# Memory keys and values between slabs of queries, W_out fetched during pooling, a fourth raw buffer, memory values in three banks, and two moves in TensorE's order

## The chip, the cores and the metric

The kernel runs on one core of one Trainium2 chip. TensorE multiplies matrices (a stationary 128x128 tile against up to 512 moving columns) into PSUM; VectorE (DVE), ScalarE (ACT) and GpSimd (POOL) do the elementwise work; SyncE (SP) issues the transfers between the chip's memory (HBM) and the core's on-chip memory (SBUF). Times are device microseconds of one execution; lower is better.

## The reference

A decoder trunk of two layers over a sequence of 1024 tokens with 1024 channels, batch 1, in float32. Both layers project the input once (W_in, 1024 to 3072 columns: main 1024, memory queries 512, main gate 1024, memory gate 512), mix, and project back (W_out, 1536 to 1024):

```python
h = x @ w_in
y_main = main_fn(u_main)                       # layer 0: pooling, layer 1: FoX
y_mem = memory_attention(q_mem, mem, w_mem_kv) # 4 heads of 128, 256 memory tokens
y = jnp.concatenate([y_main * jax.nn.silu(g_main), y_mem * jax.nn.silu(g_mem)], axis=-1)
x = layer_norm(ALPHA * x + y @ w_out, ln_g[layer], ln_b[layer])
```

The main path of layer 0 is causal pooling: four groups of 256 channels, each the trailing mean over 2, 4, 8 or 16 tokens minus the token itself, then a 256x256 map and a scale for each channel. The main path of layer 1 is forgetting attention (FoX): 16 heads of 64 channels, causal softmax over `q_t.k_s/8 + cum[t] - cum[s]`, where `cum` is the running sum of the logarithm of a forget gate. Keys, values and gates come from one more projection of the output of layer 0. Memory attention is plain cross-attention of 4 heads into 256 memory tokens, whose keys and values are projections of `mem`.

## The kernel before

Every float32 operand is split into a high and a low part (`hi_lo`, L140-143: ACT copies the rounded high part, DVE subtracts it for the low part). A product is then three matmuls: high by high, high by low, low by high. TensorE runs 7010 matmuls, most of them with 512 columns.

**Weights.** A weight piece of 128x512 (256 KB) goes by an SP transfer into a `raw` buffer (L115-116, three of them), and is split into two `w` buffers (L118, six). `split_w` (L149) does both; in the FoX stage GpSimd does the split instead of ACT and DVE (`gp_hi_lo`, L145-147, chosen by `low[0]`). A `slab` (L171) is 48 matmuls of 512 columns: it projects 1024 tokens to 128 channels, from two weight pieces, into two PSUM banks of the kind `pj`, and calls an eviction for each half. PSUM has eight banks: `pj` three, `L` two (logits), `T` two (transposes, and FoX's exponentials), `O` one (attention outputs).

**Order of the stages.** Layer 0: `pool_group(0)`; `mem_kv(0)` (L197), which projects the memory tokens to keys of four heads and then to values of four heads, 24 matmuls of 256 columns for each (`project`, 192 in a row), evicts the keys by `hi_lo` and the values by `scaled_halves` (L231), and turns the values by one transposing transfer (L228); `mem_attention(0)` (L259), which projects four slabs of queries and then runs eight query tiles; `pool_group(1)` to `(3)` (L461-504); the output projection `OutProj(0)`. Layer 1: `mem_kv(1)`, `mem_attention(1)`, then `start_units` (keys, queries, first values and forget gates of FoX), the FoX loop, and `OutProj(1)`.

**Memory attention.** For each query tile `probs` makes logits of four heads, exponentials and two half-precision halves of the probabilities (L294 is DVE's part), which a transfer turns. `values` (L302) multiplies them by the memory values for two tiles and a head in bank `O`, and DVE evicts with L310. Between those, TensorE is given pieces of gate slabs from a list, `Fill`; gate evictions are an ACT tanh and a DVE multiply (L192-195).

**Output projection.** `OutProj.load` (L335) takes 24 W_out pieces into `raw` and splits them into tiles that lie in slots that other tiles have left (`w_slots`). `rest` (L378) loads all that are missing, then goes over pairs of token tiles: 144 matmuls for each pair, in the order of the channel groups 2 (memory), 0, 1. In layer 0 all of it happens after pooling. In layer 1 the first eight pieces and the first memory products (`early`, L364) are put into the last two FoX heads.

**FoX.** The loop goes over 16 heads and eight query tiles from the longest down. For each tile GpSimd writes the causal mask into the row `R` of that head (L682; `R` is the running gate sum broadcast to all partitions, loaded by L670 from `cumd`, two buffers), TensorE makes the logits in bank `L`, DVE adds `R` and takes the running extreme (L689), ACT exponentiates (L695), one step later ACT and DVE make two halves (L712, L713), SP turns them (L722), and TensorE multiplies by the values. The spare room on TensorE is filled from `Fill` with slabs: keys, queries and values of the next pair (queries evicted by L638 and L639), and gates. At an odd head's end the list is emptied. For pair 0 the list holds gate 0, gate 1 and then `following`, the slab of pair 1's queries. In pair 7 three gates that had no room earlier come late (`late_gate`, L752: the stored output is read back, multiplied by its gate on GpSimd in one operation of 1024 columns, L756, and stored).

**Forget gates** (`forget_gates`, L594-615): DVE ends with L597; TensorE makes the running sum (L605, L607), DVE copies it, TensorE turns it (L611), SP writes `cumd` in eight transfers (L615). `start_units` (L654) steps this chain among slab matmuls.

**What sets the order.** TensorE's order in memory attention, `start_units` and the FoX loop is the program's own (`manual_schedule`). The other engines, SP and the rest of TensorE's work are ordered by a scheduler that sees the whole program; every engine runs its instructions in the order given, so an instruction that waits holds up what is behind it. SP issues all transfers in one such order.

Of the kernel before, what the change touches and what calls it, by code (L numbers as in the profile page):

```python
# [9 lines left out]
F32 = mybir.dt.float32  # L10
# [8 lines left out]
P = 128  # L19
# [6 lines left out]
MH = 4  # L26
# [45 lines left out]
def trunk_kernel(ctx, tc, x, xT, memT, win, wk, wv0, wv, wmk, wmv, wout, poolw, pscale, lng, lnb, bforget, out):  # L72
# [11 lines left out]
    for _ in range(4):  # L84
        nc.vector.memset(small.tile([P, 8], F32, tag="edge", name="edge"), 0.0)
# [29 lines left out]
    def raw(shape):  # L115
        return sb(list(shape), "raw", 3)
# [4 lines left out]
    def tiny(n, dt=F32):  # L121
        return small.tile([P, n], dt, tag=f"s{n}{dt}", name=nm("s"))
# [40 lines left out]
    edge = const.tile([P, 40], F32, name="edge")  # L163
# [33 lines left out]
    def mem_kv(l):  # L197
        mh = [T([P, 4, NMEM]) for _ in range(2)]
# [20 lines left out]
        for h in range(MH):  # L219
            hi_lo(kh[:, h, :], kl[:, h, :], project(wmk[l, h]))  # L220
        two, v = (MK([P, MH, 2 * 2, P], F16) for _ in range(2))
        undo = small.tile([P, 64], F32, tag="undo", name=nm("undo"), bufs=1)[:, :MH]
        for h in range(MH):
# [4 lines left out]
        nc.sync.dma_start_transpose(v.rearrange("p h b d -> p (h b) d"), two.rearrange("p h b t -> p (h b t)"))  # L228
        return kh, kl, v, undo
# [29 lines left out]
    def mem_attention(l, XH, XL, kv, qtile, ytile, yd):  # L259

        kh, kl, v, undo = kv
        qs = []
        for h in range(MH):
            qh, ql = qtile(), qtile()
            run(slab(win[l, 8 + h], XH, XL, lambda cols, acc: hi_lo(qh[:, cols], ql[:, cols], acc)))
            qs.append((qh, ql))
        ys, gs = [ytile() for _ in range(MH)], [G() for _ in range(MH)]
# [34 lines left out]
        def values(c, h):  # L302
            acc = ps([P, 2 * P], "O", 1)
# [23 lines left out]
    class OutProj:  # L327
# [4 lines left out]
        def __init__(self, l, wtile, yd):  # L332
            self.l, self.wtile, self.yd, self.ws, self.accs, self.n = l, wtile, yd, [{}, {}], None, 0

        def load(self, upto):  # L335

            for n in range(self.n, upto):
# [4 lines left out]
                r = raw([P, NH])  # L342
                nc.sync.dma_start(r, wout[self.l, nh, 2 * kk + j])
                hi_lo(h[j], lo[j], r)
            self.n = max(self.n, upto)
# [18 lines left out]
        def early(self, tiles):  # L364

            yh, yl = tiles
            for j in range(2):
                r, two = raw([P, 2, 2 * P]), slice(2 * j, 2 * j + 2)
                nc.sync.dma_start(r, self.yd[2, :, two, : 2 * P])
                hi_lo(yh[:, two, :], yl[:, two, :], r)  # L370

            def units():
                self.accs = self.open()
                yield from self.products(self.accs, 2, yh, yl)

            return units()

        def rest(self, resid, XH, XL, dst):  # L378
            self.load(24)
# [125 lines left out]

# [384 lines left out]
```

## Time and profile before

| | us |
|---|---|
| three runs | 1284.34, 1287.81, 1289.43 |
| median | 1287.81 |
| the profiled execution | 1289.07 |
| its span in the trace | 1287.3 |
| TensorE busy | 1251.9 (97%) |
| VectorE busy | 801.4 (62%) |
| ScalarE busy | 579.2 (45%) |
| GpSimd busy | 168.8 (13%) |

The profile is of one execution. A row of its timeline gives start, length, engine, line, operation, `out<-in`, sizes, a count, and in brackets the idle time before it and what ended that. A row of waits gives an engine and line, what it waited for, and the total, the number of times and the longest, in us. A row of windows gives a stretch, its length, the busy time of each engine with its count of instructions, the clock that TensorE was granted (1 is full), the share of time that the transfer engines were busy, and GB/s. `SPq` is SP issuing a transfer. Names of tiles such as `pj`, `L`, `O`, `raw`, `w`, `R` are those of the program. Lengths of neighbouring matmuls overlap, so the spacing of starts tells a matmul's price better than its length.

### The profile page before, as it was taken

The numbers are of one execution on the slowest core, as the hardware profiler recorded it, in microseconds if no ns is written. First come the engines' busy times: TensorE is split into PE (matmuls) and PEld (weight loads), VectorE is DVE, ScalarE is ACT, GpSimd is POOL, SyncE is SP. The second block draws the span as 40 slices with busy tenths as digits, with TensorE's granted clock in tenths as the row PEclk, the third lists the DMA queues.
The fourth block names the chain that finished last, engine by engine and source line by source line (L and its number), as shares of the span: only waits on it lengthen the run. The fifth ranks groups of instructions, "written<-read, shape, count | busy, mean of one in ns | idle before, by whom it ended". The sixth has DMA issues, their size and how long they took to land. (4 is left out here: it accounts for less than half of the span.)

```text
span 1287.3 us, 19678 instructions
## 1 busy us (share of the span) xinstructions
PE 1251.9 (97%) x7018; PEld 1036.6 (81%) x7018; DVE 801.4 (62%) x1905; ACT 579.2 (45%) x1273; POOL 168.8 (13%) x267
## 2 busy tenths in 40 slices
PE   9999999999999999999999999999999999999997
PEld 7888878888778889887887788887888777788885
DVE  6452656355565457267456777777777887674644
ACT  5332642232331124265225667766766776653110
POOL 0000000000000000000003334333334231420000
PEclk9999999999999999999999999999999999999999
DMA  6351343212474226234516866868778786986430
GB/s 221 115 148 50 92 98 114 82 56 91 158 243 137 92 91 183 64 82 112 169 47 157 160 153 162 192 143 172 171 163 185 164 187 155 230 200 200 164 115 33
DMA packets 267426, 178.65 MB, mean 139 GB/s; under 512 B 212288, under 2 KB 225728, under 8 KB 267328
## 3 DMA queue, kind: packets, MB, share of 16 engines
q1 hardware_dynamic: 267328, 177.40, 52.0%
q8 instruction: 55, 0.90, 0.3%
q14 instruction: 43, 0.35, 0.1%
HBM read 94.97 MB, written 22.61 MB: 91 GB/s over the span
## 5 line engine op out<-in xcount | busy, mean ns | idle before, releaser
L181 PE MATMUL pj<-A,w 128*128 128x512 f32 x2928 | 726.5, 396 | 1.0 <-POOL w L147 0.6
L181 PEld LDWEIGHTS pj<-A,w 128*128 128x128 f32 x2928 | 539.5, 189 | 105.8 <-ACT A L142 1.8
L143 DVE TENSOR_TENSOR w<-raw,w 128x512 fp32r<-128x512 f32 x106 | 72.9, 689 | 117.0 <-ACT w L142 115.5
L142 ACT CAST w<-raw 128x512 fp32r<-128x512 f32 x106 | 65.6, 621 | 162.4 <-PE pj L181 103.7
L695 ACT ACTIVATE T<-MK,s 128x512 f32<-128x512 f32 x192 | 110.8, 577 | 56.6 <-DVE s L689 43.3
L713 DVE SCALAR_TENSOR_TENSOR P<-T,s,P 128x512 f16<-128x512 f32 x192 | 111.5, 613 | 34.5 <-ACT P L712 32.9
L712 ACT ACTIVATE P<-T,s 128x512 f16<-128x512 f32 x192 | 102.6, 576 | 48.2 <-issue 20.9
L169 PE MATMUL L<-B,B 128*128 128x512 f32 (+3 forms) x384 | 93.1, 346 | 13.9 <-DVE s L689 11.6
L169 PEld LDWEIGHTS L<-B,B 128*128 128x128 f32 x384 | 70.0, 188 | 36.2 <-DVE s L689 20.9
L689 DVE CUSTOM_DVE_ANT_0 MK<-L,R 128x512 f32<-128x512 f32 (+3 forms) x128 | 72.9, 570 | 15.9 <-PE L L169 10.7
L601 POOL MEMSET G<- 128x128 f32 x1 | 0.2, 205 | 620.3 <-DVE V L324 620.3
L169 PEld LDWEIGHTS <-V 128*128 128x128 f16 x1152 | 65.9, 99 | 17.9 <-issue 17.4
L169 PE MATMUL O<-T,V 128*128 128x128 f16 x1152 | 77.0, 222 | 0.0
L147 POOL TENSOR_TENSOR w<-raw,w 128x512 fp32r<-128x512 f32 x54 | 69.8, 1292 | 3.9
L142 ACT CAST T<-T 128x1024 fp32r<-128x1024 f32 x23 | 24.2, 1051 | 93.4 <-DMA T<-y1d 49.3
L682 POOL TENSOR_SCALAR_AFFINE_SELECT R<-R 128x128 f32<-128x128 f32 x128 | 40.4, 318 | 190.4 <-DVE s L689 107.7
L143 DVE TENSOR_TENSOR T<-T,T 128x1024 fp32r<-128x1024 f32 x23 | 28.1, 1220 | 58.1 <-PE L L358 41.6
L146 POOL TENSOR_SCALAR w<-raw 128x512 fp32r<-128x512 f32 x54 | 36.4, 675 | 143.6 <-PE pj L181 131.7
L213 PE MATMUL pj<-T,w 128*128 128x256 f32 x384 | 48.9, 285 | 2.7 <-ACT w L142 2.1
L213 PEld LDWEIGHTS pj<-T,w 128*128 128x128 f32 x384 | 46.9, 191 | 4.3 <-ACT w L142 2.8
L358 PE MATMUL pj<-B,T 128*128 128x512 f32 x186 | 46.5, 392 | 0.8 <-DVE B L143 0.8
L358 PE MATMUL L<-B,T 128*128 128x512 f32 x174 | 42.5, 389 | 0.0
(212 smaller groups left out, 1599.9 us busy)
## 6 DMA issues: line engine op xcount, KB each, us to landing
raw<-in_win_dram SPq DMA_DIRECT2D x96, 256.0 KB, 2.7
raw<-in_wout_dram SPq DMA_DIRECT2D x48, 256.0 KB, 3.3
B<-B SPq DMA_DIRECT2D x32, 256.0 KB, 3.9
R<-cumd SPq DMA_DIRECT2D x16, 512.0 KB, 4.3
y0d<-Y SPq DMA_DIRECT2D x12, 512.0 KB, 2.7
T<-y0d SPq DMA_DIRECT2D x12, 512.0 KB, 4.3
T<-y1d SPq DMA_DIRECT2D x11, 512.0 KB, 4.5
raw<-in_wmk_dram SPq DMA_DIRECT2D x16, 256.0 KB, 2.7
```

The costliest lines, as they stand in the source:

```text
L142: nc.scalar.copy(hi, src)
L143: nc.vector.tensor_tensor(lo, src, hi.bitcast(F32), ALU.subtract)
L147: nc.gpsimd.tensor_tensor(lo, src, hi.bitcast(F32), ALU.subtract)
L169: nc.tensor.matmul(acc, a, b, start=i == 0, stop=i == len(terms) - 1)
L181: nc.tensor.matmul(accs[n], a[:, k, :], b[:, kt, n * NH : (n + 1) * NH], start=kt == 0 and i == 0, stop=kt == KT - 1 and i == 2,)
L213: nc.tensor.matmul(acc, w[:, k, :], m[pc][:, k, :], start=pc == 0 and k == 0 and i == 0, stop=pc == 1 and k == 3 and i == 2,)
L358: nc.tensor.matmul(accs[a][nh], y[:, k, a * P : (a + 1) * P], w, start=kt == 8 and i == 0, stop=kt == 7 and i == 2,)
L682: nc.gpsimd.affine_select(R[:, qs], R[:, qs], [[-1, P]], ALU.is_ge, -NEG, base=0, channel_multiplier=1)
L689: nc.vector.tensor_tensor_reduce(p[:, lo:up], lg, R[:, lo:up], 1.0, top, ALU.add, ALU.min, m[:, n : n + 1])
L695: nc.scalar.activation(e, p[:, lo:up], AF.Exp, bias=top, scale=-1.0, accum_out=sums[:, n, hd % 2, i : i + 1],)
L712: nc.scalar.activation(pair[:, lo:up], e, AF.Copy, scale=r)
L713: nc.vector.scalar_tensor_tensor(pair[:, L + lo : L + up], e, r, pair[:, lo:up], ALU.mult, ALU.subtract)
```

## The change

- `raw` has four buffers instead of three. Room comes from smaller constant tiles: four `edge` tiles and their memsets go, `tiny` tiles of 12 columns or more have two buffers, `undo` moves.
- `mem_kv` hands out `keys(h)` and `vals(h)`. In layer 0 each slab of memory queries is followed by that head's keys and values; in layer 1 all keys come first, and each slab is followed by that head's values. The turning transfer is issued after the last head's values.
- Memory `values` use bank `O` for head 1 only, and the two `T` banks for the others.
- `OutProj.load` becomes `fetch` (the transfer) and `split`. In layer 0 four pieces are split after pooling group 1, and up to twelve after groups 2 and 3, with the slots reordered: the first six tiles lie in `B` and `W`.
- In `start_units`, nine of pair 1's query matmuls come before the running sum of the gates, and 30 instead of 39 at the end.
- In pair 0 of FoX the list holds gate 0, `following`, gate 1.
- The late gates multiply on GpSimd in four pieces of 256 columns.
- In pair 7 W_out pieces are fetched ahead of their split, and `early` is stepped: two loads and two splits at steps 7, 9, 10 and 12.

```diff
     pool = ctx.enter_context(tc.tile_pool(name="pool", bufs=2))
     small = ctx.enter_context(tc.tile_pool(name="small", bufs=4))
     psum = ctx.enter_context(tc.tile_pool(name="psum", bufs=2, space=bass.MemoryType.PSUM))
-    for _ in range(4):
-        nc.vector.memset(small.tile([P, 8], F32, tag="edge", name="edge"), 0.0)
     dram = ctx.enter_context(tc.tile_pool(name="dram", bufs=1, space=bass.MemoryType.DRAM))
     count, low = [0], [False]
...
         return sb(list(shape), "MK", 4, dt)
     def raw(shape):
-        return sb(list(shape), "raw", 3)
+        return sb(list(shape), "raw", 4)
     def wt(shape):
         return sb(list(shape), "w", 6, F32R)
     def tiny(n, dt=F32):
-        return small.tile([P, n], dt, tag=f"s{n}{dt}", name=nm("s"))
+        return small.tile([P, n], dt, tag=f"s{n}{dt}", name=nm("s"), bufs=4 if n < 12 else 2)
     def w_slots(tags, where):
...
         nc.vector.memset(invc[:, t : t + 1], 1.0 / (t + 1))
     psc = const.tile([P, 8], F32, name="psc")
     pschalf = const.tile([P, 8], F32, name="pschalf")
-    edge = const.tile([P, 40], F32, name="edge")
+    edge = const.tile([P, 32], F32, name="edge")
     nc.vector.memset(edge, 0.0)
     def mm3(acc, terms):
...
         nc.vector.scalar_tensor_tensor(dst, dst, 1.0, acc, ALU.add, ALU.mult)
     def mem_kv(l):
         mh = [T([P, 4, NMEM]) for _ in range(2)]
         ml = [T([P, 4, NMEM]) for _ in range(2)]
         for q in range(4):
...
                         )
             return acc
-        for h in range(MH):
+        two, v = (MK([P, MH, 2 * 2, P], F16) for _ in range(2))
+        undo = const.tile([P, 8], F32, tag="undo", name=nm("undo"), bufs=1)[:, :MH]
+        def keys(h):
             hi_lo(kh[:, h, :], kl[:, h, :], project(wmk[l, h]))
-        two, v = (MK([P, MH, 2 * 2, P], F16) for _ in range(2))
-        undo = small.tile([P, 64], F32, tag="undo", name=nm("undo"), bufs=1)[:, :MH]
-        for h in range(MH):
+        def vals(h):
             scaled_halves(
                 project(wmv[l, h]), [two[:, h, 2 * e : 2 * e + 2, :].rearrange("p m t -> p (m t)") for e in range(2)],
                 undo[:, h : h + 1],
             )
-        nc.sync.dma_start_transpose(v.rearrange("p h b d -> p (h b) d"), two.rearrange("p h b t -> p (h b t)"))
-        return kh, kl, v, undo
+            if h == MH - 1:
+                nc.sync.dma_start_transpose(v.rearrange("p h b d -> p (h b) d"), two.rearrange("p h b t -> p (h b t)"))
+        return (kh, kl, v, undo), keys, vals
     def scaled_halves(u, halves, un, by_tile=lambda t: t):
...
     def mem_attention(l, XH, XL, kv, qtile, ytile, yd):
-        kh, kl, v, undo = kv
+        (kh, kl, v, undo), keys, vals = kv
         qs = []
+        if l:
+            for h in range(MH):
+                keys(h)
         for h in range(MH):
             qh, ql = qtile(), qtile()
             run(slab(win[l, 8 + h], XH, XL, lambda cols, acc: hi_lo(qh[:, cols], ql[:, cols], acc)))
             qs.append((qh, ql))
+            if not l:
+                keys(h)
+            vals(h)
         ys, gs = [ytile() for _ in range(MH)], [G() for _ in range(MH)]
         pt, fill = {}, Fill()
         for h in range(MH):
...
             )
         def values(c, h):
-            acc = ps([P, 2 * P], "O", 1)
+            acc = ps([P, 2 * P], *(("O", 1) if h == 1 else ("T", 2)))
             for j in range(2):
                 t = pt[2 * c + j]
                 mm3(acc[:, j * P : (j + 1) * P], [
...
         KKS = (4, 5, 0, 1, 2, 3)
         def __init__(self, l, wtile, yd):
-            self.l, self.wtile, self.yd, self.ws, self.accs, self.n = l, wtile, yd, [{}, {}], None, 0
-        def load(self, upto):
-            for n in range(self.n, upto):
+            self.l, self.wtile, self.yd, self.ws, self.accs = l, wtile, yd, [{}, {}], None
+            self.raws, self.n = [], 0
+        def fetch(self, upto):
+            while self.n + len(self.raws) < upto:
+                n = self.n + len(self.raws)
+                r = raw([P, NH])
+                nc.sync.dma_start(r, wout[self.l, n // 2 % 2, 2 * self.KKS[n // 4] + n % 2])
+                self.raws.append(r)
+        def split(self, upto):
+            while self.n < upto:
+                self.fetch(self.n + 1)
+                n = self.n
                 kk, nh, j = self.KKS[n // 4], n // 2 % 2, n % 2
                 if j == 0:
                     self.ws[nh][kk] = self.wtile(n // 2)
                 h, lo = self.ws[nh][kk]
-                r = raw([P, NH])
-                nc.sync.dma_start(r, wout[self.l, nh, 2 * kk + j])
-                hi_lo(h[j], lo[j], r)
-            self.n = max(self.n, upto)
+                hi_lo(h[j], lo[j], self.raws.pop(0))
+                self.n += 1
         def open(self, banks=(("pj", 3),) * 2 + (("L", 2),) * 2):
             accs = [ps([P, NH], *bank) for bank in banks]
...
                             )
                             yield NH
-        def early(self, tiles):
-            yh, yl = tiles
+        def early(self, yh, yl):
             for j in range(2):
                 r, two = raw([P, 2, 2 * P]), slice(2 * j, 2 * j + 2)
                 nc.sync.dma_start(r, self.yd[2, :, two, : 2 * P])
+                yield
                 hi_lo(yh[:, two, :], yl[:, two, :], r)
-            def units():
-                self.accs = self.open()
-                yield from self.products(self.accs, 2, yh, yl)
-            return units()
+                yield
+            self.accs = self.open()
+            yield from self.products(self.accs, 2, yh, yl)
         def rest(self, resid, XH, XL, dst):
-            self.load(24)
+            self.split(24)
             gb = []
             for v in (lng, lnb):
                 t = sb([P, D], "P", 4)
...
                     nc.vector.scalar_tensor_tensor(yn, acc, pschalf[:, f : f + 1], yn, ALU.mult, ALU.mult)
                 nc.sync.dma_start(y0d[f // 4, :, f % 4, :], ys[d])
+        wtags = [("B", 8)] * 4 + [("W", 4)] * 2 + [("MK", 4)] * 2 + [("Y", 4)] * 2 + [("PG", 0), ("w", 0)]
+        out_proj = OutProj(0, w_slots(wtags, in0), y0d)
         pool_group(0)
         kv = mem_kv(0)
         mem_attention(0, XH, XL, kv, bt, lambda: sb([P, S], "Y", 4, F32, in0), y0d[2])
         for g in range(1, 4):
             pool_group(g)
+            out_proj.split((4, 12, 12)[g - 1])
         XH1, XL1 = (sb([P, KT, S], "A", 2, F32R) for _ in range(2))
-        wtags = [("MK", 4)] * 2 + [("W", 4)] * 2 + [("B", 8)] * 4 + [("Y", 4)] * 2 + [("PG", 0), ("w", 0)]
-        OutProj(0, w_slots(wtags, in0), y0d).rest(x, XH1, XL1, x1)
+        out_proj.rest(x, XH1, XL1, x1)
     XH, XL = XH1, XL1
...
             for _ in v_turned():
                 yield from islice(own, 6)
             yield from own
+            yield from islice(following, 9)
             next(gates)
             yield from islice(following, 9)
             next(gates)
-            yield from islice(following, 39)
+            yield from islice(following, 30)
         def forget_rows(hd):
             R = sb([P, S], "R", 2, F32, in1)
...
             return R
         def probs(hd, i, R, sums, behind):
...
             o, g = sb([P, S], "R", 2, F32, in1), G()
             nc.sync.dma_start(o, y1d[pr // 4, :, pr % 4, :])
             yield from gate_units(win[1, 12 + pr], g, XH, XL)
-            nc.gpsimd.tensor_tensor(o, o, g, ALU.mult)
+            for c in range(4):
+                cols = slice(c * 2 * P, (c + 1) * 2 * P)
+                nc.gpsimd.tensor_tensor(o[:, cols], o[:, cols], g[:, cols], ALU.mult)
             nc.sync.dma_start(y1d[pr // 4, :, pr % 4, :], o)
         def fox(following, out_proj):
...
                             fill.add(pair_units(pr + 1), 3 * SLAB)
                         for ahead in {0: (0, 1), 2: (2,), 4: (4,), 7: (7,)}.get(pr, ()):
                             gate_ahead(ahead)
-                        if pr == 0:
-                            fill.add(following, SLAB)
+                            if ahead == 0:
+                                fill.add(following, SLAB)
                         for late in (3, 5, 6) if pr == 7 else ():
                             fill.add(late_gate(late), SLAB)
                     R, ahead_R = ahead_R, None
...
                         ahead_R = forget_rows(hd + 1)
                     if pr == 7:
                         step = b * ST + i
-                        out_proj.load(min(step + 1, 6) if step < 9 else 8)
-                        if step == 6:
-                            lead = out_proj.early([xy((P, 4, 2 * P)) for _ in range(2)])
+                        if step == 7:
+                            lead = out_proj.early(*(xy((P, 4, 2 * P)) for _ in range(2)))
+                        if step in (7, 9, 10, 12):
+                            next(lead)
+                        out_proj.split(min(step - 1, 6) if step < 14 else step - 7)
+                        out_proj.fetch(min(step + 1, 6) if step < 12 else min(step - 5, 8))
                     if hd < HEADS:
                         new = (hd, tile_of, o)
                         fresh[0] = probs(hd, tile_of, R, sums, behind)
```

## The prediction

> **What bounds the kernel now.** I read the page's busy shares first, then TensorE's waits, then the windows around each wait, then the timeline inside them.
>
> ```profile
> PE 1251.9 (97%) x7018; PEld 1036.6 (81%) x7018; DVE 801.4 (62%) x1905; ACT 579.2 (45%) x1273; POOL 168.8 (13%) x267
> ```
>
> TensorE sets the time. The change keeps every matmul, so only stalls in TensorE's order can be won. Two undisturbed rows give its steady rate:
>
> ```profile
> 81.57 43.71 PE L181 MATMUL pj<-A,w 128*128 128x512 f32 x192
> ```
> ```profile
> 491.91 17.04 PE L213 MATMUL pj<-T,w 128*128 128x256 f32 x140
> ```
>
> A 512-column matmul takes 43.71 / 192 = 0.228 us, a 256-column one 17.04 / 140 = 0.122 us. What a stretch takes beyond its matmuls at these rates is its loss. The waits of TensorE (total, times, longest, in us) name the causes:
>
> ```profile
> PE L L169 <- DVE s L689: 11.6, 13, 2.8
> PE O L169 <- DVE Y L310: 2.2, 2, 1.7
> PE pj L213 <- ACT w L142: 2.1, 2, 1.5
> PE O L169 <- DVE V L310: 1.9, 2, 1.7
> PE L L169 <- DVE B L639: 1.8, 1, 1.8
> PE O L605 <- DVE G L597: 1.7, 1, 1.7
> ```
>
> The stretches that the change touches, TensorE alone (window, length, busy, matmuls, granted clock, DMA share, GB/s). In order: memory keys and values of layer 0, of layer 1, first output projection, end of FoX pair 0, a later pair change left alone, head 14, memory values:
>
> ```profile
> 55.47:81.57 26.10, 24.06 (x193) 1.00 0.56 171
> 482.29:508.79 26.50, 25.71 (x210) 1.00 0.59 182
> 342.58:378.20 35.62, 34.37 (x146) 1.00 0.81 270
> 730.66:740.93 10.27, 8.47 (x51) 0.83 0.87 180
> 883.50:896.80 13.30, 10.74 (x55) 0.89 0.81 173
> 1118.15:1126.20 8.05, 5.29 (x28) 0.79 0.91 229
> 174.00:184.00 10.00, 8.28 (x73) 1.00 0.56 141
> ```
>
> Three of them have a clock below 1: a stall is followed there by slow matmuls, which go with it.
>
> **Part by part.**
>
> *Keys and values between slabs, layer 0.* 192 matmuls of 0.122 us are 23.4 us; the stretch takes 26.10, so 2.7 are lost. Why:
>
> ```profile
> L143 DVE TENSOR_TENSOR w<-raw,w 128x512 fp32r<-128x512 f32 x106 | 72.9, 689 | 117.0 <-ACT w L142 115.5
> L142 ACT CAST w<-raw 128x512 fp32r<-128x512 f32 x106 | 65.6, 621 | 162.4 <-PE pj L181 103.7
> ```
> ```profile
> raw<-in_wmk_dram SPq DMA_DIRECT2D x16, 256.0 KB, 2.7
> ```
> ```profile
> 75.23 0.50 PE L213 MATMUL pj<-T,w 128*128 128x256 f32 x2 [1.46 <-ACT w L142]
> ```
>
> A raw buffer is held for 2.7 us of landing, 0.62 of ACT and 0.69 of DVE, 4.0 in all; three buffers give a piece per 1.34 us. A projection uses two pieces in 24 x 0.122 = 2.9 us, 1.46 per piece: no slack for ACT and DVE to be late. After the change a slab (48 x 0.228 = 10.9 us) and two projections use six pieces in 16.8 us, 2.8 per piece. Bounds: -2.7 to 0. I take **-2.7**, since supply is then twice the demand. The transpose of the values on SP comes behind more weight loads, but the first use of the values is some 20 us of matmuls later in the order, so it costs nothing; without that cover it would cost its own few us.
>
> *Fourth raw buffer, layer 1.* Keys stay in a row there, values go between slabs.
>
> ```profile
> 483.24 1.06 PE L252 MATMUL T<-ident,G 128*128 128x128 f32 x8
> 484.06 4.44 PE L213 MATMUL pj<-T,w 128*128 128x256 f32 x32
> 489.09 1.92 PE L213 MATMUL pj<-T,w 128*128 128x256 f32 x12 [0.59 <-ACT w L142]
> ```
>
> 16 transposes at 1.06 / 8 are 2.1 us, so 26.50 - 23.4 - 2.1 = 1.0 us is lost here, 0.59 of it in this wait. Four buffers supply a piece per 1.0 us against 1.46. Bounds -1.0 to 0 (ACT also has the layer norm's transposes to evict): **-0.7**.
>
> *Memory values in three banks.* All L310 waits add up to 2.2 + 1.9 = 4.1 us.
>
> ```profile
> 178.82 1.17 PE L181 MATMUL pj<-A,w 128*128 128x512 f32 x4
> 181.71 0.83 PE L169 MATMUL O<-T,MK 128*128 128x128 f16 x12 [1.72 <-DVE Y L310]
> ```
> ```profile
> 179.60 1.67 DVE L294 SCALAR_TENSOR_TENSOR P<-P,s,P 128x256 f16<-128x256 f32 x4
> 181.19 0.48 DVE L310 TENSOR_SCALAR Y<-O,undo 128x256 f32<-128x256 f32 x1
> ```
>
> The bank was full at 178.82 and emptied at 181.67, 2.9 us later, because L310 queued behind L294. With banks T, O, T the fourth head waits only for the first head's eviction; between lie two heads with their fill, 2 x (0.83 + 1.17) = 4.0 us, and a further 1.17. The other banks' users (the transposes, FoX's exponentials) aren't live here. Bounds -4.1 to 0: **-4.0**.
>
> *W_out during pooling.* 342.58 to 378.20 holds 144 matmuls (146 less one overlapping at each edge), 32.8 us; 2.8 are lost. Twelve of 24 pieces, those used first, are loaded and split earlier: 12 x 0.62 ACT and 12 x 0.69 DVE, 7.4 and 8.3 us. The cover:
>
> ```profile
> 290.00:340.00 50.00, 49.85 (x220) 41.02 (x219) 27.97 (x44) 14.08 (x22) 0.00 (x0) 1.00 0.29 90
> ```
>
> (PE, PEld, DVE, ACT, POOL.) In this last pooling stretch DVE is idle for 22 us, ACT for 36, DMA share 0.29. The thirteenth to sixteenth go to MK slots that pooling's last matmuls (to 342.58) still read; they take 4 x 1.34 = 5.4 us and are first used 54 matmuls, 12.3 us, later; the last eight follow from 22 us on. Bounds -2.8 to +1 (an eviction of pooling behind two splits, 1.3): **-2.4**.
>
> *Cumulative gates: nine matmuls of pair 1 ahead of them.* The G L597 wait of 1.7 goes. What is late next is row R:
>
> ```profile
> 671.79 0.46 PE L605 MATMUL O<-G,G 128*128 128x128 f32 x2 [1.65 <-DVE G L597]
> ...
> 681.93 0.81 SPq L670 DMA_DIRECT2D R<-cumd  x2
> ...
> 687.14 0.69 DVE L689 CUSTOM_DVE_ANT_0 MK<-L,R 128x512 f32<-128x512 f32 x1 [0.93 <-DMA R<-cumd]
> ```
>
> 9 x 0.228 = 2.05 us end just when L597 does, so L605 starts no earlier, and cumd, R and L689 stay where they are. TensorE reaches FoX's first logits about 2 us sooner and waits there instead. Bounds 0 to +2 (a longer single wait, then slow matmuls): **+0.5**.
>
> *Pair 1's queries between gates 0 and 1.*
>
> ```profile
> 736.16 1.59 PE L169 MATMUL L<-B,B 128*128 128x512 f32 x4 [1.80 <-DVE B L639]
> ```
> ```profile
> 738.61 0.29 POOL L682 TENSOR_SCALAR_AFFINE_SELECT R<-R 128x128 f32<-128x128 f32 x1 [2.42 <-DMA R<-cumd]
> ```
>
> The pair's first logits waited for its query's eviction, issued last. Of the window's 10.27 us, 22 matmuls of 512 columns are 5.0 and 24 small ones, at the 0.83 / 12 of the values above, 1.7: 3.6 lost, half in the wait, half in the slow clock behind it. Earlier queries remove the wait, but GpSimd's mask of the next head, in order ahead of this head's next one, still waits for R at 738.61. Bounds -3.6 to -1.0: **-2.5**. The second gate's evictions now come last; no logits wait for them.
>
> [...]
>
> *Piece at 1088.*
>
> ```profile
> 1088.39 0.97 PE L181 MATMUL pj<-A,w 128*128 128x512 f32 x3 [0.63 <-POOL w L147]
> ```
>
> SP's load of this piece moves ahead of the value transposes: -0.6, bounds -0.9 to +0.9 (a W_out load ahead of it instead).
>
> *Head 14: fetch ahead, split later, early tiles in steps.*
>
> ```profile
> 1118.83 0.62 ACT L142 CAST B<-raw 128x512 fp32r<-128x512 f32 x1 [3.91 <-DMA raw<-in_wout_dram]
> ```
> ```profile
> 1121.53 0.51 PE L169 MATMUL L<-B,B 128*128 128x256 f32 x2 [2.76 <-DVE s L689]
> ```
>
> ACT stood 3.91 us behind a W_out transfer; L712, L713, L689 and TensorE (2.76) queue behind it. 8.05 us hold ten matmuls of 512 columns, two of 256 and 14 to 16 values, 3.6 us by the rates above: 4.5 lost. With the transfer issued at least two steps before its split, the wait goes; the split itself (0.62, 0.69) stays ahead of head 15's first exponentials. Bounds -4.5 to +2 (a split, its DVE half and the exponential behind it, still late): **-2.5**.
>
> *The rest.* Four pieces instead of one multiply on GpSimd (13% busy), at most some tenths; four memsets less: 0.
>
> Sum: -2.7 -0.7 -4.0 -2.4 +0.5 -2.5 -0.6 -2.5 = **-14.9 us**. The profiled execution took 1289.07 (span 1287.3 and 1.77 around it), 1.3 over the median 1287.81: 1274.2 on its own basis, 1272.9 on the median's. Say **1273**.
>
> **Rivals.**
>
> *A. The gains from 670 us on come back as R waits.* In FoX, L689 is already the largest wait (11.6 us), and
>
> ```profile
> POOL R L682 <- DMA R<-cumd: 54.2, 15, 8.8
> ```
>
> shows GpSimd behind R at nearly every head. If the cumulative-gate term is +2 and the last three are nothing, the sum is -2.7 -0.7 -4.0 -2.4 + 2 = -7.8: 1280. Against it: the waits at 736 and 1118 end by L639 and by a W_out transfer, not by R.
>
> *B. The changed orders make R the last wait at more heads: slower.* At 883.50 to 896.80 a change of head takes 13.3 us for 26 matmuls of 512 columns, six of 384 or fewer and some 20 values, 8.3 us: 5.0 lost, with clock 0.89. FoX has 15 changes of head; each that newly stalls so costs 5.0. Five of them give 1273 + 25 = 1298, and it is slower than now by over 0.5% (1294.2) from 21.2 / 5.0, the fifth, on. For it: GpSimd waits for R 15 times; against: only pair 0 and pair 7 change order, and between them the sequence of heads, loads and masks stays.
>
> *C. The transfers weren't the limit.* If the piece supply hangs on ACT's and DVE's queues and not on buffers, the terms of keys, W_out and head 14 go, -0.6 with them: -4.0 + 0.5 - 2.5 = -6.0, some 1282. Against: ACT's idle time names the DMA in head 14.
>
> **How the numbers follow.** This kernel's measurement can tell about 0.5%, 6.4 us. My forecast 0.57, A 0.22, C 0.11, B 0.10. The forecast's own range is 1268 (every term at its gaining bound, -2.7 - 1.0 - 4.1 - 2.8 - 3.6 - 0.9 - 4.5 = -19.6) to 1279; the range given reaches over A and C, and 3 us below for the spread of the runs: 1265 to 1284. Faster, that is under 1281.4: the forecast and 0.17 of A, 0.74; same: 0.05 of A and C, 0.16; slower: B, 0.10.
>
> **What would show it.** In the changed profile: no L213 wait on L142 over 0.5 us and 48 512-column matmuls between projections without a gap; no L310 waits; the first output projection's first 24 matmuls per bank in 5.5 us each; L605 without a wait, L689 at FoX's start still waiting for R with TensorE idle about 3 us; no L639 wait at the first pair change; no ACT wait on W_out of several us in head 14. I am wrong if these stalls are gone and L L169's waits on L689 grow by more than they save, or if pooling's evictions wait behind the W_out splits.

## The result and the profile after

The changed kernel takes 1276.09 us (median of six runs, 1273.81 to 1281.01) against 1286.81 before (six runs, 1284.33 to 1289.87): the medians lie 10.7 us apart, and the ratio is 0.9921, 95% interval 0.9895 to 0.9947. The profiled execution took 1275.16 with a span of 1273.4; it is 0.9 below its median, where the profiled one of before (1289.07) was 2.3 above. The page's busy row and the first waits of TensorE (total, times, longest, us) after the change; lines have moved (L143 is now L141, L181 L179, L169 L167, L213 L212, L310 L319, L358 L376, L597 L615, L639 L657, L689 L709, L739 L759):

```profile
PE 1243.5 (98%) x7018; PEld 1032.7 (81%) x7018; DVE 803.8 (63%) x1901; ACT 578.5 (45%) x1273; POOL 174.2 (14%) x276
```
```profile
PE L L167 <- DVE s L709: 14.1, 15, 3.1
PE idle L92 <- DVE warm L89: 1.3, 1, 1.3
PE O L167 <- DVE G L759: 1.1, 1, 1.1
PE pj L179 <- ACT A L140: 0.8, 2, 0.4
PE pj L212 <- DVE w L141: 0.8, 1, 0.8
```

Gone are the waits on the values' eviction (L310, 4.1), on the memory weights' ACT half (2.1), on the query eviction (L639, 1.8) and on the gates (L597, 1.7). The wait on L709 has grown from 11.6 to 14.1, and one on L759 is new. TensorE alone in the stretches that answer to those of before: layer 0's queries, keys and values; first output projection; layer 1's keys; memory values; end of FoX pair 0; head 14; and the last output projection's start:

```profile
56.77:123.39 66.62, 66.62 (x386) 1.00 0.36 102
337.59:370.27 32.68, 32.68 (x146) 1.00 0.69 230
474.50:500.00 25.50, 24.50 (x160) 1.00 0.49 156
171.67:178.03 6.36, 6.36 (x66) 1.00 0.52 112
706.34:716.00 9.66, 9.21 (x57) 1.00 0.52 113
1093.00:1109.00 16.00, 12.28 (x71) 0.89 0.75 197
1135.00:1157.00 22.00, 19.32 (x86) 1.00 0.84 294
```

The first, second and fourth have no idle time left. Layer 1's keys, the end of pair 0 (0.45 us), head 14 and the last output projection have.

To compare runs I took every start of a matmul in each trace, subtracted the median spacing of its form, and added up what is beyond, place by place. A single place leaves out groups of small excesses under about 0.4 us, except at the memory values; the last row has everything. In us lost:

| place | before | after | after, second profile |
|---|---|---|---|
| start of the program | 1.6 | 2.7 | 3.6 |
| keys and values, layer 0 | 3.1 | 0 | 0 |
| memory values, both layers | 8.1 | 2.9 | 2.9 |
| end of pooling, first output projection | 3.1 | 0 | 0 |
| keys, layer 1 | 1.9 | 1.9 | 1.9 |
| gates and FoX's first logits | 3.5 | 1.9 | 1.3 |
| end of pair 0 | 4.4 | 1.2 | 1.2 |
| pair changes 770 to 1064 us | 12.9 | 10.8 | 11.5 |
| pair 7 and head 14 | 10.4 | 9.3 | 7.9 |
| last output projection | 0 | 3.8 | 3.1 |
| whole program | 55.8 | 42.2 | 40.6 |

The 2.9 us at the memory values are eight groups of about 0.35 us each, which stand in every run whatever the banks. Part of the difference between the traces is the clock: the trace of before has four stretches inside the program at half the clock, the first trace after has one, from 1105.00 to 1108.40.

```profile
736.79:740.20 3.41, 3.41 (x16) 0.50 0.88 214
893.80:897.21 3.41, 3.41 (x13) 0.50 0.71 129
1081.54:1084.94 3.40, 3.40 (x10) 0.50 0.56 128
1122.50:1125.90 3.40, 3.40 (x20) 0.50 1.10 223
```

Each costs at most half its length, 1.7 us, so up to 5 of the 13.6 us between these two traces are clock. Over all executions the mean granted clock is 0.995 before and after, so the medians don't owe their difference to it.

Two profiles of the same program differ by up to 2 us at one place, so a difference of that size between two traces is read as a cause below only where rows show it.

### The profile page after: what moved, and what is told of

Its sections match the earlier page's. It is cut to its first block, busy times and chain, and to the rows that moved or that the text cites. A ratio compares the mean times of both kernels' runs of the same rounds, so it can differ in the third digit from the quotient of the medians.

```text
span 1273.4 us, 19681 instructions
## 1 busy us (share of the span) xinstructions
PE 1243.5 (98%) x7018; PEld 1032.7 (81%) x7018; DVE 803.8 (63%) x1901; ACT 578.5 (45%) x1273; POOL 174.2 (14%) x276
## 5 line engine op out<-in xcount | busy, mean ns | idle before, releaser
L179 PE MATMUL pj<-A,w 128*128 128x512 f32 x2928 | 723.4, 395 | 0.8 <-ACT A L140 0.8
L179 PEld LDWEIGHTS pj<-A,w 128*128 128x128 f32 x2928 | 536.5, 188 | 103.9 <-ACT A L140 2.4
L141 DVE TENSOR_TENSOR w<-raw,w 128x512 fp32r<-128x512 f32 x106 | 74.0, 700 | 105.9 <-ACT w L140 105.1
L167 PE MATMUL L<-B,B 128*128 128x512 f32 (+3 forms) x384 | 92.0, 344 | 14.5 <-DVE s L709 14.1
L167 PEld LDWEIGHTS L<-B,B 128*128 128x128 f32 x384 | 69.8, 188 | 36.8 <-DVE s L709 23.9
L709 DVE CUSTOM_DVE_ANT_0 MK<-L,R 128x512 f32<-128x512 f32 (+3 forms) x128 | 72.9, 570 | 12.0 <-PE L L167 7.2
L167 PEld LDWEIGHTS <-V 128*128 128x128 f16 x1152 | 65.2, 99 | 18.6 <-issue 18.6
L167 PE MATMUL O<-T,V 128*128 128x128 f16 x1152 | 76.2, 221 | 1.1 <-DVE G L759 1.1
L141 DVE TENSOR_TENSOR T<-T,T 128x1024 fp32r<-128x1024 f32 x23 | 28.1, 1223 | 70.2 <-PE L L376 51.3
L144 POOL TENSOR_SCALAR w<-raw 128x512 fp32r<-128x512 f32 x54 | 35.8, 664 | 139.9 <-PE pj L179 131.3
L212 PE MATMUL pj<-T,w 128*128 128x256 f32 x384 | 48.7, 284 | 0.9 <-DVE w L141 0.8
L212 PEld LDWEIGHTS pj<-T,w 128*128 128x128 f32 x384 | 47.6, 192 | 2.0 <-DVE w L141 1.3
L376 PE MATMUL pj<-B,T 128*128 128x512 f32 x186 | 46.5, 392 | 0.5 <-DVE T L141 0.5
L376 PE MATMUL L<-B,T 128*128 128x512 f32 x174 | 43.0, 391 | 0.0
```

Of the source, the lines that this page charges most:

```text
L141: nc.vector.tensor_tensor(lo, src, hi.bitcast(F32), ALU.subtract)
L167: nc.tensor.matmul(acc, a, b, start=i == 0, stop=i == len(terms) - 1)
L179: nc.tensor.matmul(accs[n], a[:, k, :], b[:, kt, n * NH : (n + 1) * NH], start=kt == 0 and i == 0, stop=kt == KT - 1 and i == 2,)
L212: nc.tensor.matmul(acc, w[:, k, :], m[pc][:, k, :], start=pc == 0 and k == 0 and i == 0, stop=pc == 1 and k == 3 and i == 2,)
L376: nc.tensor.matmul(accs[a][nh], y[:, k, a * P : (a + 1) * P], w, start=kt == 8 and i == 0, stop=kt == 7 and i == 2,)
L709: nc.vector.tensor_tensor_reduce(p[:, lo:up], lg, R[:, lo:up], 1.0, top, ALU.add, ALU.min, m[:, n : n + 1])
```

## The experiments

Each is the changed kernel with one edit, unless said otherwise. Ratios are to the kernel before, run beside it.

| run | median, us | ratio | 95% interval |
|---|---|---|---|
| unaltered again | 1275.31 | 0.9935 | 0.9913 to 0.9956 |
| three raw buffers | 1276.24 | 0.9943 | 0.9923 to 0.9962 |
| pair 7's W_out as before | 1275.36 | 0.9938 | 0.9916 to 0.9961 |
| layer 0's W_out after pooling | 1278.24 | 0.9959 | 0.9941 to 0.9977 |
| values in one bank | 1280.06 | 0.9957 | 0.9941 to 0.9972 |
| keys and values of layer 0 in a row | 1274.96 | 0.9919 | 0.9903 to 0.9934 |
| gates' running sum at its old place | 1276.15 | 0.9928 | 0.9911 to 0.9944 |
| pair 1's queries after both gates | 1278.14 | 0.9943 | 0.9925 to 0.9960 |
| W_out staged in the output projection | 1273.88 | 0.9917 | 0.9900 to 0.9933 |
| no W_out in pair 7 before step 12 | 1270.43 | 0.9882 | 0.9862 to 0.9902 |
| both of the last two | 1267.03 | 0.9870 | 0.9851 to 0.9890 |
| both, three raw buffers | 1273.30 | 0.9912 | 0.9896 to 0.9927 |

The theory was that each part removes the stall at its own place and that the gain reaches the end; the rivals were that R's chain takes it back in FoX, and that the transfers were not the limit. The first run is the measure for the others:

> The changed kernel once more, unaltered. All theories: 1276 within 3 us, and TensorE's stalls at the same places and within 0.5 us each of the first profile (3.8 us and 2.5 us around head 14, 2.2 and 1.6 in the last output projection, 1.9 at FoX's start). A stall that differs by more than 1 us between the two profiles is no evidence for a cause of that size.

Most places agree (last column above), but the start, FoX's start, the pair changes, pair 7 and the last output projection don't within the 0.5 us that I expected: they differ by 0.6 to 1.4.

**Layer 0's keys: buffers or spacing?**

```diff
-        return sb(list(shape), "raw", 4)
+        return sb(list(shape), "raw", 3)
```

> The change with three raw buffers instead of four, all else kept. Theory spacing (what took the stalls away in layer 0 is that pieces are asked for every 2.8 us instead of every 1.46): no stall returns at keys and values of layer 0 nor in the first output projection, 1275 to 1277, and the start's extra 1.1 us may go. Theory buffers (the fourth buffer does it): 2 to 3 us return at the keys and 1 to 3 in the first output projection, 1280 to 1282.

```diff
         for h in range(MH):
...
-            if not l:
-                keys(h)
-            vals(h)
+            if l:
+                vals(h)
```

(with layer 0's four `keys` and four `vals` ahead of the loop)

> Keys and values of layer 0 in a row again ahead of the queries, with the four raw buffers kept. Theory spacing: 2 to 3 us of stalls among the 192 matmuls return, 1278 to 1279. Theory buffers (supply of a piece per 1.0 us against a demand of 1.46 is enough): under 0.7 us, 1276. Layer 1, whose keys are in a row with four buffers and which still lost 1.9 us, speaks for some return.

With three buffers and the new spacing nothing is lost at the keys; with four buffers and the old row nothing is lost either (ratio 0.9919, no slower than the unaltered kernel's 0.9935). Each of the two edits alone removes these 3 us, so together they win them once. The fourth buffer shows elsewhere: with three, pair 7 and head 14 lose 12.1 us instead of 7.9 to 9.3, and the last output projection 0 instead of 3.1 to 3.8. Of the 12.1 us, 5.0 are one wait of TensorE for a gate's weight piece, which GpSimd splits (L144) when its transfer has landed. The fourth buffer wins in one place about what it costs in the other, and the time is the same.

**W_out of layer 0.**

```diff
-            out_proj.split((4, 12, 12)[g - 1])
```

> Layer 0's W_out is again loaded only after pooling; all else kept. Theory local (a stall that an edit removed comes back at its place and reaches the end): 2.5 to 3.2 us return in the first output projection, 1279 within 1.5. Rival spill (what one stage wins is lost further on): under 1 us, 1276 to 1277. With the fourth raw buffer the returning stall may be smaller, 1 to 2 us.

1.5 us come back where pooling ends and nothing inside the output projection, the smaller of the sizes I gave for a fourth buffer. Of the 3.1 us won here, half stays won without the early pieces. With them and only three buffers (the run with three raw buffers) nothing is lost here either: the early pieces alone are enough, and what they add to the fourth buffer is 1.5 us.

**Banks.**

```diff
-            acc = ps([P, 2 * P], *(("O", 1) if h == 1 else ("T", 2)))
+            acc = ps([P, 2 * P], "O", 1)
```

> Memory values in one bank again, all else kept. Theory local, sized by waits: 4.1 us of waits on their eviction return, 1280. Theory local, sized by starts: the stretches around the values lose all they lost before over the steady rate, 7.1 us against 0.4, so 6.7 return, 1282 to 1283. Theory spill: less than 2 us reaches the end, 1277 to 1278.

The waits are back, in the same size as before:

```profile
PE O L167 <- DVE Y L319: 2.0, 2, 1.7
PE O L167 <- DVE V L319: 1.9, 2, 1.7
```

These are 3.9 us; by the starts of the matmuls 7.7 are lost around the values instead of 2.9, so 4.8 come back. The 6.7 us that I had expected by the starts (7.1 less 0.4) were too many: where a stall joined one of the groups of about 0.35 us I had counted the group, and where none did I had left it out. The profile counts a wait only where TensorE stands idle in its rows; matmuls whose rows overlap the wait probably hide the rest, which no run tests. The ratio is above those of the three runs beside it (0.9919 to 0.9943) by 2 to 5 us, and the median 4 to 5 us above the two of the changed kernel: that speaks against 6.7, and doesn't tell 3.9 from 4.8.

**Running sum of the gates.**

```diff
-            yield from islice(following, 9)
             next(gates)
             yield from islice(following, 9)
             next(gates)
-            yield from islice(following, 30)
+            yield from islice(following, 39)
```

> The running sum of the gates at its old place, all else kept. Theory R (the row R sets FoX's first masks, so TensorE waits there whatever comes before): the wait for the gates of about 1.8 us is back, the wait at FoX's first logits is shorter by as much, the end at 1276 within 0.7. Theory local: FoX's start loses 3.5 us in both places instead of 1.3 to 1.9, so 1.6 to 2.2 return, 1278.

3.6 us are lost at the two places instead of 1.3 to 2.0 in the other runs: theory local, by the profile; the times (1276.15 against 1276.09 and 1275.31) don't show it. R's chain didn't stay where it was. In this run, GpSimd's split of a weight piece, SP's next weight load, SP's load of R, and the first mask addition:

```profile
661.10 0.46 PE L623 MATMUL O<-G,G 128*128 128x128 f32 x2 [1.64 <-DVE G L615]
...
669.33 1.29 POOL L145 TENSOR_TENSOR w<-raw,w 128x512 fp32r<-128x512 f32 x1
...
670.65 0.35 SPq L149 DMA_DIRECT2D raw<-in_win_dram  x1
...
671.25 0.81 SPq L688 DMA_DIRECT2D R<-cumd  x2
...
676.54 0.69 DVE L708 CUSTOM_DVE_ANT_0 MK<-L,R 128x512 f32<-128x512 f32 x1 [1.01 <-DMA R<-cumd]
```

In the changed kernel:

```profile
661.93 0.38 PE L623 MATMUL O<-G,G 128*128 128x128 f32 x2
...
668.04 1.29 POOL L145 TENSOR_TENSOR w<-raw,w 128x512 fp32r<-128x512 f32 x1
...
670.19 0.37 SPq L149 DMA_DIRECT2D raw<-in_win_dram  x1
...
671.27 0.34 SPq L689 DMA_DIRECT2D R<-cumd  x1
...
676.29 0.69 DVE L709 CUSTOM_DVE_ANT_0 MK<-L,R 128x512 f32<-128x512 f32 x1 [0.69 <-DMA R<-cumd]
```

From the running sum to the first L709 it is 676.29 - 661.93 = 14.4 us, with the sum at its old place 676.54 - 661.10 = 15.4. With the sum at its old place SP's weight load starts at 670.65, just as GpSimd's split ends (669.33 + 1.29), and R's load stands behind it. With nine matmuls moved ahead that split is over at 669.33, and R's load waits only until `cumd` has landed. SP's waits from 669 to 672 us, first with the sum at its old place, then in the changed kernel:

```profile
SPq L149 <- POOL w L145: 1.2, 1, 1.2
```
```profile
SPq L689 <- DMA cumd<-G: 0.5, 1, 0.5
```

That accounts for 1 us; for the rest of the 1.6 to 2.3 I have no row.

**Queries of pair 1.**

```diff
-                            if ahead == 0:
-                                fill.add(following, SLAB)
+                        if pr == 0:
+                            fill.add(following, SLAB)
```

> Pair 1's queries after both gates again, all else kept. Theory local: the stall at the first pair change is back with its slow clock, 3.5 to 3.9 us against 0.8, so about 3 return, 1279. Theory R: GpSimd's wait for the next head's R holds the pair change anyway, and under 1.5 return, 1277.

```profile
723.43 1.19 PE L167 MATMUL L<-B,B 128*128 128x512 f32 x4 [1.79 <-DVE B L657]
```
```profile
717.90:728.20 10.30, 8.51 (x58) 1.00 0.93 182
```

The same wait as before the change, 1.79 after 1.80, but the granted clock of the stretch is 1.00 where it was 0.83, and 2.6 us are lost at the end of pair 0 instead of 4.4. What comes back over the changed kernel's 1.2 is about 1.3. So this part is worth 1.3 us without a slow clock and 3 with one.

**Pair 7.**

```diff
-                        out_proj.split(min(step - 1, 6) if step < 14 else step - 7)
-                        out_proj.fetch(min(step + 1, 6) if step < 12 else min(step - 5, 8))
+                        out_proj.split(min(step + 1, 6) if step < 9 else 8)
```

(and both early loads with their splits at step 6)

> Only the schedule of W_out and of the early tiles in FoX's last pair is put back as before; late gates in four pieces stay. Theory held buffers (with fetch ahead of split the four raw buffers are all held, transfers are issued no earlier, and W_out's splits now sit ahead of evictions at the end): head 14 loses 4.7 us instead of 6.3 and the 3.8 us in the last output projection go, 1271 within 2. Rival order (the end's 3.8 us come from SP's order of the token loads, whatever pair 7 does): 1274 to 1276 with 3.8 still there. Rival gain (fetching ahead does pay): 1278 or more.

9.7 us are lost in pair 7 and head 14, and 3.1 in the last output projection: the schedule of W_out in pair 7 changes neither. Rival order holds for the end, and fetching ahead wins nothing. Rows of the changed kernel show where it is lost (DVE, SP, ACT, TensorE):

```profile
1091.81 1.71 DVE L141 TENSOR_TENSOR B<-raw,B 128x512 fp32r<-128x512 f32 x1
```
```profile
1093.94 0.86 SPq L350 DMA_DIRECT2D raw<-in_wout_dram  x2
```
```profile
1098.41 1.32 ACT L140 CAST B<-raw 128x512 fp32r<-128x512 f32 x2 [3.87 <-DMA raw<-in_wout_dram]
```
```profile
1102.82 0.73 PE L167 MATMUL L<-B,B 128*128 128x512 f32 x2 [3.11 <-DVE s L709]
```

SP issues the next two pieces only at 1093.94, and ACT waits 3.87 us for the first, as it waited 3.91 before; TensorE's wait of 3.11 follows. Two things hold the issue back. DVE's last split before it, which gives a raw buffer back, ends only at 1091.81 + 1.71 = 1093.52. And SP itself stands in its order: three transposes come first, for which it waits on TensorE, and in SP's waits from 1088 to 1097 us none is one of L350 for a buffer:

```profile
SPq L742 <- PE pj L179: 2.2, 1, 2.2
SPq L742 <- PE L L167: 1.1, 1, 1.1
```

So at the moment of issue it was SP's order that held the transfer; how much sooner the buffers would have let it go isn't shown. Two edits for this and for the end:

```diff
+                        if step >= 12:
+                            out_proj.split(2 * (step - 11))
-                        out_proj.split(min(step - 1, 6) if step < 14 else step - 7)
-                        out_proj.fetch(min(step + 1, 6) if step < 12 else min(step - 5, 8))
```

> In FoX's last pair no W_out piece is loaded or split in its first twelve steps; eight come in the last four. Theory transfers (TensorE's stalls of 8 to 11 us from pair 7's start to the middle of head 14 come from ACT waiting for W_out): at most 5 us stay there, 1271 to 1272 if the end doesn't pay, 1274 if the last steps do. Rival masks (GpSimd's masks, R and the late gates' weights hold it): 8 us or more stay, 1275 to 1277.

```diff
         def rest(self, resid, XH, XL, dst):
-            self.split(24)
...
                 nc.sync.dma_start(src, self.yd[c, :, :, sp * 2 * P : (sp + 1) * 2 * P])
+                self.split({2: 8, 0: 16, 1: 24}[c])
                 hi_lo(yh, yl, src)
```

> The output projection asks for W_out in three parts, eight, sixteen and twenty-four pieces ahead of the channel groups 2, 0 and 1, with each group's load of tokens ahead of its part, instead of all twenty-four first. Theory queue (the 3.1 to 3.8 us lost in the last output projection with four raw buffers come from W_out pieces ahead of the token loads on SP and of the last evictions on ACT): they go, 1272 to 1273. Rival banks (they come from one O bank and its late eviction at the end of FoX): over 2.5 us stay, 1275 to 1276.

> Both edits. Under theories queue and transfers: 1267 to 1270, the sum of what each wins. If only one holds, that one's time. If the end pays for the late pieces (eight splits on ACT and DVE in the last four steps are 8 x 1.3 us of elementwise work), 1275 or more.

Without W_out before step 12, 3.7 us are lost in pair 7 and head 14 instead of 7.9 to 9.3, so theory transfers holds as it was put; the edit takes away ACT's waits for W_out and the splits themselves, and doesn't tell which of the two counts for more. The last output projection then pays 4.7. With the staged loads 1.3 are lost there, so theory queue holds for most of it. Its rows in the changed kernel: first ACT splits a late W_out piece ahead of the last heads' eviction (L758), and TensorE waits 1.11 us for the bank; then ACT takes two W_out pieces ahead of the tokens, and TensorE waits for the tokens' halves.

```profile
1138.43 0.62 ACT L140 CAST R<-raw 128x512 fp32r<-128x512 f32 x1 [1.99 <-DMA raw<-in_wout_dram]
1139.07 0.47 ACT L758 ACTIVATE G<-O,unscale 64x256 f32<-64x256 f32 x1
```
```profile
1140.35 0.50 PE L167 MATMUL O<-T,V 128*128 128x128 f16 x6 [1.11 <-DVE G L759]
```

```profile
1149.58 0.62 ACT L140 CAST B<-raw 128x512 fp32r<-128x512 f32 x1 [5.90 <-DMA raw<-in_wout_dram]
```
```profile
1153.50 1.05 ACT L140 CAST T<-T 128x1024 fp32r<-128x1024 f32 x1 [1.72 <-DMA T<-y1d]
```
```profile
1154.60 0.73 PE L376 MATMUL T<-MK,T 128*128 128x512 f32 x2 [0.52 <-ACT T L140]
```

Both edits together lose 3.7 and 1.4, at full clock, in pair 7 with head 14 and at the end:

```profile
1066.00:1113.00 47.00, 45.71 (x272) 1.00 0.84 195
1135.00:1157.00 22.00, 21.47 (x94) 1.00 0.68 236
```

At 1267.03 this version beats both kernels: 0.9870 of the one before.

**Is the fourth buffer needed then?** The same with three:

> The version with staged W_out in the output projection and none in FoX's last pair before step 12, but with three raw buffers. Theory W_out only (the fourth buffer mattered in FoX's last pair because W_out pieces held buffers there; elsewhere wider spacing of demand is enough): 1267 within 1.5, no new stall over 1 us. Rival everywhere (gate weights, first output projection and the end need the fourth buffer as well): 2 to 5 us return in FoX's last pair or in the output projections, 1269 to 1272.

```profile
PE O L167 <- DVE G L759: 5.6, 1, 5.6
```

Pair 7 and head 14 stay low (3.9 us), but one wait of 5.6 us for the last heads' eviction stands at the end, with slow matmuls after it (clock 0.84 from 1135 to 1157 us): 1273.30, so rival everywhere is nearer. ACT's rows, with three buffers and then with four:

```profile
1134.91 1.04 ACT L140 CAST T<-T 128x1024 fp32r<-128x1024 f32 x1 [9.11 <-DMA T<-y1d]
1135.98 0.47 ACT L758 ACTIVATE G<-O,unscale 64x256 f32<-64x256 f32 x1
```
```profile
1128.54 0.47 ACT L758 ACTIVATE G<-O,unscale 64x256 f32<-64x256 f32 x1 [1.40 <-PE O L167]
```

With three buffers ACT was given the split of the tokens first, stood 9.11 us before it, and the eviction (L758) had to wait; with four the eviction came first. What returned is an order on ACT, not a wait for a raw buffer. Whether three buffers would do with the eviction put first wasn't tried.

## Why the prediction was right, and where it was not

The time, 1276.1, is 3 us above the 1273 forecast and within its range; 10.7 us were won for 14.9 forecast. The likeliest case held in kind: the stalls on L310, L639, L597 and the memory weights' ACT half are gone, and FoX didn't give back what layer 0 won. By term:

- *Keys and values, layer 0: -2.7.* 3.1 won. The reason given, supply at twice the demand, leaned on the wider spacing; either the spacing or the fourth buffer alone is enough.
- *Fourth buffer, layer 1: -0.7.* Nothing won: 1.9 before and after, and 1.9 or 2.0 in every run, with three buffers too. The step that failed is that a quicker supply of raw pieces ends this wait: TensorE waits for DVE's half, and DVE has layer norm's operations ahead of it:

```profile
481.65 1.58 PE L212 MATMUL pj<-T,w 128*128 128x256 f32 x11 [0.80 <-DVE w L141]
```
```profile
478.95 0.74 DVE L436 SCALAR_TENSOR_TENSOR G<-G,s,P 128x512 f32<-128x512 f32 x1
...
479.69 0.73 DVE L436 SCALAR_TENSOR_TENSOR G<-G,s,P 128x512 f32<-128x512 f32 x1
```

- *Three banks: -4.0.* 4.8 by the starts in the run with one bank, 5.2 between the two traces. The mechanism was right; the term, the sum of the profile's waits, was about 1 us too small.
- *W_out during pooling: -2.4.* 3.1 won at that place; the early pieces alone win it, the fourth buffer alone would win half.
- *Running sum of the gates: +0.5.* About -2. The step that failed is "cumd, R and L689 stay where they are": before, R's load stood behind a weight load for which SP waited 0.7 us on GpSimd; now the first L709 comes 1 us sooner after the running sum.
- *Pair 1's queries: -2.5.* 3.2 between the two profiles, 1.3 at equal clock. R didn't hold the pair change.
- *Piece at 1088 and head 14: -3.1.* 10.4 lost before, 9.3 and 7.9 after, 9.0 to 11.5 in the other runs with four buffers and this schedule. The step that failed is "with the transfer issued at least two steps before its split, the wait goes": the program asked earlier, but SP issued the pieces no earlier against ACT's need, behind transposes and a late buffer, and ACT still waited 3.87 us.
- *Not in the sum:* 3.1 to 3.8 lost in the last output projection. It appears with four buffers and not with three. The prediction counted a fourth buffer only as supply; it also lets W_out pieces get ahead of the tokens on SP and ACT.

The measured terms are -3.1, 0, -4.8, -3.1, -2, -1.3 to -3.2, about -1 and +3.1 to +3.8, which makes -11.5 to -14.1; the start of the program, which no term had, lost 1.1 and 2.0 us more in the two traces after. The traces after lose 13.6 and 15.2 us less than that of before; the medians show 10.7. The profiled execution of before was one of its slower ones (1289.07; the medians of later runs are 1283.19 to 1285.36), with the four stretches at half clock. That the total came within 3 us of the forecast is in part luck: terms that won too little (layer 1's keys, head 14, the end) were offset by others that won more than forecast.

Rival A failed: the terms from 670 us on were not all lost, and where one was, in head 14, ACT's wait names a W_out transfer and not R. Rival B did not come: the pair changes between 770 and 1064 us lost 12.9 before, with one of the stretches at half clock (893.80), and 10.8 to 11.5 after. Of rival C the part on head 14 holds in effect, though for another reason: the transfers are late there, but asking for them two steps ahead didn't start them in time.

## What to carry to other kernels

An earlier place in program order didn't make a transfer come sooner here: ACT waited 3.87 us for it after 3.91 before. The last split before it ended at 1093.52, SP stood behind three transposes, and it was issued at 1093.94. So ask whether a buffer is free by then and whether the issuing engine is held by what stands ahead, and count everything that draws on the same pool. Another number of buffers also changed what comes first on ACT: with three, the last heads' eviction stood behind a split that waited 9.11 us, with four it came first. So ask what a transfer or a split will overtake. And the profile's sum of waits can be too small for a stall (here 3.9 for 4.8): take the spacing of starts, and the clock behind it, apart.

## What the hardware showed beyond that

The same wait at the same place was followed by slow matmuls in the kernel before (1.80 us, clock 0.83) and by none in the run with pair 1's queries after both gates (1.79 us, clock 1.00); one of 1.72 us at the memory values of the kernel before left the clock at 1.00 as well. So the length of the wait alone didn't settle it; what does isn't shown. Ahead of each stretch at half clock inside the program, TensorE was busy for 0.97 to 1.72 us of the 3.41 before it, first in the kernel before, then in the changed one:

```profile
733.37:736.79 3.42, 1.62 (x8) 1.00 0.65 170
890.39:893.80 3.41, 1.56 (x7) 1.00 0.38 98
1078.13:1081.54 3.41, 1.71 (x7) 1.00 0.26 65
1119.09:1122.50 3.41, 0.97 (x5) 1.00 0.62 189
```
```profile
1101.59:1105.00 3.41, 1.72 (x7) 1.00 0.57 191
```

DVE's subtraction of 512 columns took 0.69 us in the mean row of before, but 1.71 at 1091.81, beside GpSimd's own subtraction, which took 1.60 where it took 1.29 at 668.04:

```profile
1091.37 1.60 POOL L145 TENSOR_TENSOR w<-raw,w 128x512 fp32r<-128x512 f32 x1
```

In the two traces before and after, every one of DVE's subtractions of this size that overlaps none of GpSimd's operations took 0.63 to 0.70 us; those that overlap one took 0.67 to 2.01. Why some of these took longer isn't shown. The extra 1.0 us lies in head 14 ahead of DVE's other work there; what it costs wasn't tried.
